# Weight loads moved to ScalarE's queue and gated-head stores to GpSimd's queue in a differential-attention layer

## The chip, the cores and the metric

The kernel runs on one core of one Trainium2 chip. The core has five engines that each run their own list of instructions in order: TensorE (PE in the profile), VectorE (DVE), ScalarE (ACT), GpSimd (POOL) and SyncE (SP). A transfer between HBM and on-chip memory is started by an instruction in one of these lists, and is then carried out by 16 DMA engines. An instruction that waits for a semaphore holds everything behind it in the same list. The metric is the device time of one execution in microseconds (us); lower is better.

## What is computed

One layer of gated differential attention, for 1024 tokens, width 1024, 16 heads of 128 columns each (two maps of 64), in float32:

```python
h = rms_norm(x, norm_g)
q, k, v, z = jnp.split(h @ w_in, 4, axis=-1)
q = rms_norm(q.reshape(b, s, DA_HEADS, 2, DA_HEAD), q_norm_g) * (DA_HEAD ** -0.5)
k = rms_norm(k.reshape(b, s, DA_HEADS, 2, DA_HEAD), k_norm_g)
...
    probs = jax.nn.softmax(scores + bias[None, :, None], axis=-1)
    weights = probs[:, :, 0] - lam * probs[:, :, 1]
    outs.append(jnp.einsum('bhqk,bkhe->bqhe', weights.astype(v.dtype), vb))
...
o = rms_norm(o, head_norm_g) * (1.0 - lam_0)
o = o.reshape(b, s, BRANCH) * jax.nn.silu(z)
return x + o @ w_out
```

`scores` is causal with a linear bias by distance.

## The kernel before

Float32 products are made from float16 pairs: each operand is split into a high and a low part, and three matmuls (high x high, high x low, low x high) stand for one.

The kernel works head by head, in the order of `heads`: the eight odd heads, then the eight even ones. For each head, `project` makes queries, keys and values (`gemm_piece`, L365 to L367: eight pieces of 128 tokens, each in one of three PSUM banks of the pool `ps_g`) and the gate (`gate`, L442 to L452, two halves `c` of 512 tokens; z is stored in a buffer `sz`, of which there are three). Heads 10, 12 and 14 (`LATE`) get their gates in `late_gates` at the end. At the same time, `attend` does the attention of the head before: eight steps of `scores`, each for 128 queries and 128 to 1024 keys (matmuls L564; VectorE takes the scores from PSUM with a running minimum, L553; ScalarE takes the exponential, L570; VectorE combines the two maps, L573 to L576; ScalarE and VectorE split the result, L66 and L580; a transposing transfer L582 on SyncE's queue turns it for `values`). `merge` interleaves the two lists by estimated TensorE time.

The weights of a head come from `w_in` in `load_raw`: eight transfers (`L135`), one for each 128 rows, into the buffer `raww`, of which there is one. A transfer is 256 KB for four blocks (q, k, v, z) and 192 KB for three. `split_w` then takes each block's largest square on ScalarE (L159), finds a scale, and splits: ScalarE writes the high part (L197); VectorE the low part of q and k (L203); GpSimd that of v and z (L200 scales in place, L201 subtracts). So the load for the next head can only start when the last L201 has read `raww`.

A finished half of a head (`finalize`) is gated on GpSimd (`L532`), or on VectorE for the late heads, and is stored to `g_dram` (`L533`, 256 KB). That store frees the `sz` buffer, for which a later `L447` waits. At the end the heads are read back and multiplied by `w_out` (L493 to L499).

A scheduler orders each engine's list when the program is built, by a simulated timeline; instructions that `pin` or `keep_in_program_order` marks keep their place. So moving a transfer to another queue also changes the order around it.

Of the kernel before, what the change touches and what calls it, by code (L numbers as in the profile page):

```python
# [39 lines left out]
def diff_attention_kernel(  # L40
# [18 lines left out]
    V, A, G, T, Q = nc.vector, nc.scalar, nc.gpsimd, nc.tensor, nc.sync  # L59
# [22 lines left out]
    g_dram = [dram.tile([4, P, NH, P], F32, name=f"g_dram{c}") for c in range(2)]  # L82
# [22 lines left out]
    heads = [h for h in range(NH) if h % 2 == 1] + [h for h in range(NH) if h % 2 == 0]  # L105
    place = {h: i for i, h in enumerate(heads)}

    with ExitStack() as main:
# [16 lines left out]
        def load_raw(hd, raw=None, blocks=None):  # L125


            if blocks is None:
                blocks = range(3 if isinstance(hd, slice) or hd in LATE else 4)
            if raw is None:  # L130
                raw = wr.tile([P, KT, 4, P], F32, name="raww", tag="raww")
            for k in range(KT):
                rows = wq_view[k * P:(k + 1) * P]
                bs = slice(blocks[0], blocks[-1] + 1)
                ins = Q.dma_start(raw[:, k, bs], rows[:, 3, hd] if isinstance(hd, slice) else rows[:, bs, hd])  # L135
                if hd == heads[0]:
                    tc.keep_in_program_order(ins)
            return raw, blocks
# [75 lines left out]
        with ExitStack() as pro:  # L214
# [12 lines left out]
            load_x()  # L227
            A.dma_start(gb, bcast(norm_g))
            raw0 = load_raw(heads[0], None, range(3))[0]
            load_x()  # L230
            load_x()
# [35 lines left out]
            for t in range(NB):  # L267
                ht = hts[t]
                c, o = t // 4, (t % 4) * P
# [7 lines left out]
                if t == 0:  # L277
                    for _ in range(KT + 1):
                        next(w0)
                    hts.append(chain(1))  # L280
                    for _ in w0:
                        pass
                    load_raw(heads[0], raw0, range(3, 4))
# [65 lines left out]
        def project(hd, wt, st):  # L349
# [46 lines left out]
            if nx is not None:  # L396
                st["wt"] = {}
                prep.append(split_w(*load_raw(nx), st["wt"], nx))
# [106 lines left out]
        def late_gates(sts, wt):  # L505
            for c in range(2):
                wo = wo_half(0, wr, "rawo", 2) if c else None
                if c:
                    g01 = qkp.tile([P, 2, 2, 4, P], F32R, name="gt01", tag="qk")
                    for q in range(2):  # L510
                        raw = tmp.tile([P, 4, 2, P], F32, name="rawg", tag="rw", bufs=2)
                        first.update(split_g(g01[:, q], raw.rearrange("p a b e -> p (a b) e"), 0, q))
                for n, (hd, st) in enumerate(sts):
                    for k in gate(st, wt, n, c):
                        if c == 1 and k % 3 == 0:
                            next(wo, None)
                        yield 0.64
                    if n < len(sts) - 1:
                        finalize(hd, c, st["t"][c], st["z"][c])
            yield from part_block(tmp.tile([P, 1024], F32, name="xr0", tag="sqk", bufs=2)[:, :512], 0, 0, first)  # L520
# [3 lines left out]
        def finalize(hd, c, t1, z):  # L524
            if hd == heads[-1]:
                V.tensor_tensor(t1, t1, z, ALU.mult)
                gs = glast[c]
                V.tensor_scalar(gs[0], t1, 1.0, None, ALU.mult)
                V.tensor_tensor(gs[1], t1, gs[0].bitcast(F32), ALU.subtract)
                return  # L530
            e = V if hd in LATE else G
            e.tensor_tensor(z, t1, z, ALU.mult)  # L532
            Q.dma_start(g_dram[c][:, :, place[hd], :].rearrange("t p e -> p t e"), z.rearrange("p (t e) -> p t e", t=4))  # L533

        def attend(hd, st):

# [73 lines left out]
            def head_norm(c):  # L610
                os, sq, sqh, sql = pos["n"]
                pm_ = ps_o.tile([P, 512], F32, name="pmn", tag="po")
                T.matmul(pm_, ones, sqh, start=True, stop=False)
                T.matmul(pm_, ones, sql, start=False, stop=True)
                yield 0.43
                A.activation(sq, pm_, AF.Ln, bias=eps_t)
                A.activation(sq, sq, AF.Exp, scale=-0.5)
                if hd in LATE[:-1]:
                    nm = ("whz", "wlz")[c]
                    t1 = wzp.tile([P, 512], F32, name="t1", tag=nm)  # L620
                    st["t"].append(t1)
                    V.scalar_tensor_tensor(out=t1, in0=os, scalar=gh, in1=sq, op0=ALU.mult, op1=ALU.mult)
                else:
                    V.scalar_tensor_tensor(out=sq, in0=os, scalar=gh, in1=sq, op0=ALU.mult, op1=ALU.mult)  # L624
                    finalize(hd, c, sq, st["z"][c])
# [36 lines left out]
        for i in range(NH + 1):  # L662
            att = None
            if i > 0:
                hd, stp = prev
# [81 lines left out]
```

## Time and profile before

| | us |
|---|---|
| median of three runs (1170.47 to 1178.97) | 1173.36 |
| the profiled execution's own time | 1169.15 |
| its span in the trace | 1167.4 |
| TensorE busy (95% of the span) | 1109.9 |
| VectorE busy (78%) | 906.5 |
| ScalarE busy (64%) | 751.7 |
| GpSimd busy (23%) | 269.7 |

Busy time does not count instructions that start transfers or wait. In a row of the timeline the first number is the start in us from the span's start, the second the time in us; "[1.02 <-DVE v_k L95]" is the idle time of that engine just before the row, and what ended it. SPq and ACTq are the lists of SyncE and ScalarE where they start transfers. The middle of the trace, from about 170 to 870 us, repeats with each head, about 58 us for one.

### The profile page before, as it was taken

To read this page: it belongs to the slowest core of one execution; us is meant where nothing else is said; L and a number is where in the kernel's file an instruction comes from. 1 tells how busy PE (TensorE), PEld (TensorE's weight loads), DVE (VectorE), ACT (ScalarE), POOL (GpSimd) and SP (SyncE) were. 2 spreads that over 40 slices of the span, in tenths; PEclk is the share of its full clock that TensorE was granted. 3 is DMA by queue.
4 is the path that set the end of the run, shared out by engine and by line. 5 is a ranking of instruction groups with operands and counts; after the bars stand their busy time and mean duration, and the time that the engine had idled before them with its cause. 6 is when DMAs were issued, how large, how long until landed. Compare 5 with 4: busy or idle time off the path is not lost.

```text
span 1167.4 us, 18462 instructions
## 1 busy us (share of the span) xinstructions
PE 1109.9 (95%) x6154; PEld 670.2 (57%) x6154; DVE 906.5 (78%) x2336; ACT 751.7 (64%) x1585; POOL 269.7 (23%) x208
## 2 busy tenths in 40 slices
PE   4999999999899999999999999999999988999998
PEld 3655554555455555554545555555555535788887
DVE  6868968898879898989888989797898898554121
ACT  4757678686868686868686868686768766230000
POOL 2221313131413131314131313212120402022000
PEclk7999999999999999999999999999999988999999
DMA  6352636354636364635473635353664456766341
GB/s 222 109 118 57 147 82 143 81 125 96 142 84 141 86 144 83 150 77 145 82 150 77 147 80 136 79 142 70 138 136 91 116 112 160 193 235 227 113 131 70
DMA packets 327887, 143.50 MB, mean 123 GB/s; under 512 B 225136, under 2 KB 307312, under 8 KB 327792
## 3 DMA queue, kind: packets, MB, share of 16 engines
q1 hardware_dynamic: 323040, 133.93, 47.8%
q10 hardware_dynamic: 4752, 8.39, 2.6%
q8 instruction: 48, 0.79, 0.3%
q14 instruction: 47, 0.39, 0.1%
HBM read 63.11 MB, written 16.25 MB: 68 GB/s over the span
## 4 chain that ended last, share of the span: by engine, by line
PE 53%; DVE 15%; ACT 11%; DMA 7%; issue 6%; POOL 4%; SPq 4%; ACTq 0%; DVEq 0%; POOLq 0%
PE pg L365 8%; PE pg L366 8%; PE pg L367 8%; PE pf L493 5%; PE pf L494 5%; PE pf L495 5%; DMA raww<-in_l_w_in_dram 4%; DVE p L553 4%; SPq L135 3%; PE pss L564 3%; ACT wsp L197 3%; ACT wsp L159 3%; POOL wsp L201 2%; ACT p L570 2%; DVE p L576 2%
## 5 line engine op out<-in xcount | busy, mean ns | idle before, releaser
L365 PE MATMUL pg<-wsp,h 128*128 128x384 f16 x1024 | 336.1, 328 | 12.8 <-DVE sz L452 7.7
L366 PE MATMUL pg<-wsp,h 128*128 128x384 f16 x1024 | 336.1, 328 | 1.2 <-POOL wsp L201 1.2
L367 PE MATMUL pg<-wsp,h 128*128 128x384 f16 x1024 | 336.0, 328 | 0.9 <-DVE h L276 0.9
L570 ACT ACTIVATE p<-p,mn 128x128 f32<-128x128 f32 (+7 forms) x256 | 196.6, 769 | 36.1 <-DVE mn L553 36.0
L564 PE MATMUL pss<-qk 128*128 128x512 f16 (+3 forms) x768 | 165.9, 327 | 18.5 <-DVE mn L553 18.5
L553 DVE CUSTOM_DVE_ANT_0 p<-pss,toep,nsl 128x512 f32<-128x512 f32 (+3 forms) x256 | 161.3, 643 | 17.7 <-DMA wt<-p 8.2
L66 ACT ACTIVATE p<-p,rc 128x128 f16<-128x128 f32 (+7 forms) x128 | 98.8, 773 | 77.6 <-DVE p L576 71.7
L366 PEld LDWEIGHTS <-h 128*128 128x128 f16 x1024 | 100.8, 98 | 77.3 <-issue 17.2
L367 PEld LDWEIGHTS <-h 128*128 128x128 f16 x1024 | 100.8, 98 | 68.7 <-issue 4.0
L365 PEld LDWEIGHTS <-h 128*128 128x128 f16 x1024 | 100.7, 98 | 65.9 <-issue 3.7
L580 DVE SCALAR_TENSOR_TENSOR p<-p,rc,p 128x128 f16<-128x128 f32 (+7 forms) x128 | 109.1, 853 | 10.2 <-ACT p L66 9.4
L564 PEld LDWEIGHTS <-qk 128*128 128x128 f16 x768 | 70.8, 98 | 78.6 <-issue 26.6
L576 DVE SCALAR_TENSOR_TENSOR p<-p,rc,p 128x128 f32<-128x128 f32 (+7 forms) x128 | 108.7, 854 | 0.0
L607 POOL TENSOR_TENSOR sql<-sqo,sqh 128x512 fp32r<-128x512 f32 x30 | 41.0, 1366 | 263.2 <-ACT sqh L605 263.2
L442 PE MATMUL pz<-h,wsp 128*128 128x512 f16 x256 | 98.1, 383 | 1.8 <-DVE sz L452 1.8
L444 PE MATMUL pz<-h,wsp 128*128 128x512 f16 x256 | 98.1, 383 | 0.0
L443 PE MATMUL pz<-h,wsp 128*128 128x512 f16 x256 | 98.1, 383 | 0.0
L200 POOL TENSOR_SCALAR raww<-raww,scw 128x1024 f32<-128x1024 f32 (+1 forms) x31 | 43.5, 1410 | 178.4 <-ACT wsp L197 137.2
L532 POOL TENSOR_TENSOR sz<-sqo,sz 128x512 f32<-128x512 f32 x26 | 33.7, 1295 | 184.9 <-DVE sqo L624 165.4
L159 ACT ACTIVATE wsp<-raww 128x1024 f16<-128x1024 f32 x61 | 63.7, 1045 | 19.3 <-DMA raww<-in_l_w_in_dram 14.9
L553 DVE CUSTOM_DVE_ANT_0 p<-pss,toep,mn 128x128 f32<-128x128 f32 (+3 forms) x128 | 75.4, 603 | 0.3 <-PE pss L564 0.3
L201 POOL TENSOR_TENSOR wsp<-raww,wsp 128x1024 f16<-128x1024 f32 (+1 forms) x31 | 71.7, 2327 | 0.5
(159 smaller groups left out, 2048.7 us busy)
## 6 DMA issues: line engine op xcount, KB each, us to landing
raww<-in_l_w_in_dram SPq DMA_DIRECT2D x96, 256.0 KB, 4.3
rawo<-in_l_w_out_dram SPq DMA_DIRECT2D x32, 256.0 KB, 4.7
qk<-qk SPq DMA_DIRECT2D x64, 128.0 KB, 2.3
raww<-in_l_w_in_dram SPq DMA_DIRECT2D x40, 192.0 KB, 3.6
g_dram<-sz SPq DMA_DIRECT2D x30, 256.0 KB, 2.2
rawg<-g_dram ACTq DMA_DIRECT2D x24, 256.0 KB, 4.0
xt<-in_x_dram SPq DMA_DIRECT2D x8, 512.0 KB, 5.2
xr<-in_x_dram SPq DMA_DIRECT2D x16, 256.0 KB, 3.5
```

The source lines that it names most:

```text
L66: A.activation(out, in_, AF.Copy, scale=scale)
L159: A.activation(hi[:, :, s_], raw[:, :, s_], AF.Square, accum_out=bd[:, j:j + 1])
L365: T.matmul(pg, a_h, w_h, start=k == 0, stop=False)
L366: T.matmul(pg, a_h, w_l, start=False, stop=False)
L367: T.matmul(pg, a_l, w_h, start=False, stop=k == KT - 1)
L442: T.matmul(pz, wt["hi"][:, k, n], hh[c][:, k], start=k == 0, stop=False)
L443: T.matmul(pz, wt["hi"][:, k, n], hl[c][:, k], start=False, stop=False)
L553: V.tensor_tensor_reduce(out=pm[m][:, o:o + w], in0=pss[:, :w], in1=toep[:, u:u + w], scale=nslope, scalar=3e38 if prev[m] is None else pr ...
L564: T.matmul(pss[m][:, :w].rearrange("p (t q) -> p t q", q=P), qk[:, c, 0, i % 4, m], qk[:, b, v, :w // P, m], start=v == 1, stop=v == 2)
L570: A.activation(pm[m][:, :n], pm[m][:, :n], AF.Exp, scale=-1.0, bias=prev[m], accum_out=sx[:, m:m + 1])
L576: V.scalar_tensor_tensor(out=p0, in0=p1, scalar=rc[:, 1:2], in1=p0, op0=ALU.mult, op1=ALU.add)
L580: V.scalar_tensor_tensor(out=pl[:, n:], in0=p0, scalar=rc[:, 0:1], in1=pl[:, :n], op0=ALU.mult, op1=ALU.subtract)
```

## The change

Loads of `w_in` for all heads but the first are started by ScalarE (`A`) in place of SyncE (`Q`): 16 groups of eight transfers, 128 in all (96 of 256 KB, 32 of 192 KB; the last group holds the gate weights of the three late heads). The 30 stores of gated heads are started by GpSimd (`G`).

```diff
-                ins = Q.dma_start(raw[:, k, bs], rows[:, 3, hd] if isinstance(hd, slice) else rows[:, bs, hd])
+                ins = (Q if hd == heads[0] else A).dma_start(raw[:, k, bs], rows[:, 3, hd] if isinstance(hd, slice) else rows[:, bs, hd])
...
-            Q.dma_start(g_dram[c][:, :, place[hd], :].rearrange("t p e -> p t e"), z.rearrange("p (t e) -> p t e", t=4))
+            G.dma_start(g_dram[c][:, :, place[hd], :].rearrange("t p e -> p t e"), z.rearrange("p (t e) -> p t e", t=4))
```

ScalarE's list in the middle of the program, where the fifth attended head is at its seventh step (896 keys; `p_4107` and `p_4108` are the two maps' scores). Before:

```order
L570 ACTIVATE p_4107,sx<-p_4107,mn 128x896
L570 ACTIVATE p_4108,sx<-p_4108,mn 128x896
L97 ACTIVATE y_k<-v_k 128x16
L98 ACTIVATE y_k<-y_k 128x16
L447 ACTIVATE sz<-pz,inv 128x512
L66 ACTIVATE p_4108<-p_4107,rc 128x896
L449 ACTIVATE sz<-sz 128x512
```

The same place in ScalarE's list after the change:

```order
L570 ACTIVATE p_4107,sx<-p_4107,mn 128x896
L135 DMA raww<-in_l_w_in_dram 128x4x128 x2
L570 ACTIVATE p_4108,sx<-p_4108,mn 128x896
L135 DMA raww<-in_l_w_in_dram 128x4x128 x2
L97 ACTIVATE y_k<-v_k 128x16
L447 ACTIVATE sz<-pz,inv 128x512
L135 DMA raww<-in_l_w_in_dram 128x4x128
L98 ACTIVATE y_k<-y_k 128x16
L135 DMA raww<-in_l_w_in_dram 128x4x128 x2
L66 ACTIVATE p_4108<-p_4107,rc 128x896
L449 ACTIVATE sz<-sz 128x512
L135 DMA raww<-in_l_w_in_dram 128x4x128
```

Two of the eight loads now stand between the two exponentials of the step, and six more among the short operations behind them.

A little further in ScalarE's list (the gate's last exponential L451, the squares L159 of the weights just loaded, and L386, a part of the key's and query's split). Before:

```order
L386 ACTIVATE sqk<-rw 128x16x64
L617 ACTIVATE sqo<-sqo 128x512
L159 ACTIVATE wsp,bd<-raww 128x8x128 x3
L451 ACTIVATE sz<-sz 128x512
L159 ACTIVATE wsp,bd<-raww 128x8x128
L570 ACTIVATE p_4273,sx<-p_4273,mn 128x128
```

After:

```order
L617 ACTIVATE sqo<-sqo 128x512
L451 ACTIVATE sz<-sz 128x512
L159 ACTIVATE wsp,bd<-raww 128x8x128 x4
L386 ACTIVATE sqk<-rw 128x16x64
L570 ACTIVATE p_4273,sx<-p_4273,mn 128x128
```

L451 now comes ahead of all four squares, and L386 behind them.

VectorE's list at the first of these places (`rc` comes from the sums `sx` of the two exponentials; `p_4195` is the next step). Before:

```order
L553 ISA p_4108,mn<-pss,toep,mn,nsl 128x384
L553 ISA mn 128x1
L95 TENSOR_SCALAR v_k<-ssk,ep 128x8 x2
L573 RECIPROCAL rc<-sx 128x2
L553 ISA p_4195,mn<-pss,toep,nsl 128x512
L553 ISA mn 128x1
```

After:

```order
L553 ISA p_4108,mn<-pss,toep,mn,nsl 128x384
L553 ISA mn 128x1
L580 SCALAR_TENSOR_TENSOR p_3996<-p_3995,rc,p_3996 128x768
L95 TENSOR_SCALAR v_k<-ssk,ep 128x8 x2
L553 ISA p_4195,mn<-pss,toep,nsl 128x512
L553 ISA mn 128x1
L573 RECIPROCAL rc<-sx 128x2
```

L573, which needs both exponentials, now stands behind the next step's first L553.

In SyncE's list only the transposing transfers L582 and L388 and the copies L391 are left in the middle of the program. On GpSimd each L533 stands right behind its L532.

## Rows read from the trace of the kernel before

**Rows 1.** The page, busy us of each engine, share, instructions.

```profile
PE 1109.9 (95%) x6154; PEld 670.2 (57%) x6154; DVE 906.5 (78%) x2336; ACT 751.7 (64%) x1585; POOL 269.7 (23%) x208
```

**Rows 2.** Windows: stretch, length, busy PE, PEld, DVE, ACT, POOL, then clock, DMA.

```profile
0.00:100.00 100.00, 77.65 (x440) 48.83 (x441) 71.12 (x214) 60.66 (x141) 22.33 (x25) 0.88 0.49 136
...
170.00:870.00 700.00, 679.49 (x3966) 380.95 (x3965) 604.68 (x1606) 534.64 (x1130) 181.40 (x122) 1.00 0.51 114
870.00:1167.00 297.00, 282.81 (x1338) 200.37 (x1336) 172.27 (x372) 107.34 (x210) 47.78 (x50) 0.97 0.52 146
```

**Rows 3.** Waits of PE, 170 to 870 us: total us, times, longest.

```profile
PE pss L564 <- DVE mn L553: 9.8, 10, 1.6
PE pg L365 <- DVE sz L452: 7.3, 8, 1.9
```

**Rows 4.** Waits of DVE and of ACT for transfers, 170 to 870 us.

```profile
DVE p L553 <- DMA wt<-p: 5.0, 5, 2.2
...
ACT sz L447 <- DMA g_dram<-sz: 2.8, 4, 1.4
```

**Rows 5.** Waits of SyncE's queue, whole span: total us, times, longest.

```profile
SPq L533 <- POOL sz L532: 109.0, 17, 10.2
...
SPq L135 <- POOL wsp L201: 61.7, 16, 7.4
```

**Rows 6.** Lines L135, L533, L479: time to issue, ns min/median/max, first and last.

```profile
L135 SPq DMA_DIRECT2D raww<-in_l_w_in_dram x144: 328/622/2157, 1.2 to 871.4; - x144
...
L533 SPq DMA_DIRECT2D g_dram<-sz x30: 364/382/993, 124.8 to 992.0; - x30
...
L479 ACTq DMA_DIRECT2D rawg<-g_dram x32: 326/326/1071, 902.2 to 1138.9; - x32
```

**Rows 7.** Landing of the stores L533, us from issue, min/median/max.

```profile
DMA to landing us min/median/max: 2.2/2.2/3.5
```

**Rows 8.** Timeline of SyncE's queue, one head in the middle.

```profile
363.63 5.46 SPq L135 DMA_DIRECT2D raww<-in_l_w_in_dram  x8
...
379.64 0.54 SPq L533 DMA_DIRECT2D g_dram<-sz  x1
```

**Rows 9.** Timeline of POOL, the same head.

```profile
358.66 4.94 POOL L201 TENSOR_TENSOR wsp<-raww,wsp 128x1024 f16<-128x1024 f32 x2
...
376.64 1.27 POOL L532 TENSOR_TENSOR sz<-sqo,sz 128x512 f32<-128x512 f32 x1 [10.57 <-DVE sqo L624]
```

**Rows 10.** Timeline of ACT, the same head.

```profile
361.00 1.04 ACT L570 ACTIVATE p<-p,mn 128x896 f32<-128x896 f32 x1
...
362.73 1.04 ACT L570 ACTIVATE p<-p,mn 128x896 f32<-128x896 f32 x1 [0.59 <-DVE mn L553]
...
373.77 1.06 ACT L159 ACTIVATE wsp<-raww 128x1024 f16<-128x1024 f32 x1
...
376.91 0.61 ACT L451 ACTIVATE sz<-sz 128x512 f32<-128x512 f32 x1
...
382.21 0.69 ACT L447 ACTIVATE sz<-pz,inv 128x512 f32<-128x512 f32 x1
```

**Rows 11.** Timeline of DVE, the same head, behind the two exponentials.

```profile
364.77 0.15 DVE L573 RECIPROCAL rc<-sx 128x2 f32<-128x2 f32 x1
364.84 0.73 DVE L553 CUSTOM_DVE_ANT_0 p<-pss,toep,nsl 128x512 f32<-128x512 f32 x1
```

**Rows 12.** Timeline of PE, the same head, its only waits.

```profile
377.01 1.02 PE L564 MATMUL pss<-qk 128*128 128x512 f16 x4 [0.78 <-DVE mn L553]
378.36 0.32 PE L365 MATMUL pg<-wsp,h 128*128 128x384 f16 x1 [0.32 <-DVE sz L452]
```

**Rows 13.** Timeline of ACT and then PE, first head.

```profile
51.36 1.06 ACT L159 ACTIVATE wsp<-raww 128x1024 f16<-128x1024 f32 x1 [1.64 <-DMA raww<-in_l_w_in_dram]
...
56.06 0.19 ACT L97 ACTIVATE y_x<-v_x 128x1 f32<-128x1 f32 x1
...
59.66 0.66 PE L273 MATMUL tp<-ident,htok 128*128 128x128 f32 x2 [2.13 <-DVE htok L257]
```

## The prediction, made before the changed kernel was run

> **What bounds the kernel now.** I read the page's busy times first. TensorE works 1109.9 of 1167.4 us [rows 1], so a change of loads and stores can win only what TensorE stands still. The windows say where that is [rows 2]: in the middle, 170 to 870 us, TensorE works 679.49 of 700 us, so 20.5 us of idle time in all lie there; in the first 100 us it is idle for 22.35, in the last 297 for 14.2. The column for VectorE shows the second limit: 604.68 of 700 us in the middle (86%), ScalarE 534.64 (76%), GpSimd only 181.40 (26%). An engine that gets later by a microsecond is therefore not at once on the path, but VectorE has little room.
>
> Then the waits, for what the moved transfers hold up. TensorE in the middle waits 9.8 us for VectorE's running minimum L553 (`mn`) and 7.3 us for VectorE's L452, which frees a bank of the gate [rows 3]; the rest up to 20.5 is short pieces. None of the two is a wait for a transfer. VectorE waits 5.0 us for transposed weights and ScalarE 2.8 us for a store of a gated head, both in the middle [rows 4]. SyncE's own queue does wait much: 109.0 us in 17 waits at the stores L533, for GpSimd's L532, and 61.7 us in 16 waits at the loads L135, for GpSimd's last L201 [rows 5]. These are the waits that the change removes from SyncE. But behind them only [rows 4] shows anyone late, 5.0 + 2.8 us, and those two are not the bound.
>
> **The loads, on ScalarE.** 128 loads move in 16 groups of eight. On SyncE eight of four blocks took 5.46 us to issue [rows 8], 0.68 us each. With 192 KB in place of 256 I take 0.51 by the ratio. The total is 96 x 0.68 + 32 x 0.51 = 82 us of a second queue's time, 5.1 us a group. ScalarE, 76% busy in the middle, has 165 us left there, so the sum fits; the question is where in its list it lies.
>
> Take the head at 361 us. GpSimd's two L201 run from 358.66 for 4.94 us and so end at 363.60 [rows 9]. ScalarE ran the first 896-key exponential from 361.00 to 362.04, waited 0.59 us for VectorE and ran the second from 362.73 to 363.77 [rows 10]. In the new list two loads stand between them (the first order rows in the section on the change). They wait for L201, till 363.60, then take 2 x 0.68 = 1.37 us; the second exponential runs from 364.97 to 366.01, 2.2 us later. Queued behind the wait are this exponential, then the key norm's L97, L447, L66 and L449; of these the exponential is wanted first. VectorE's L573 needs both exponentials' sums. Before, it ran at 364.77, ahead of the 512-key L553, which ended at 364.84 + 0.73 = 365.57 [rows 11]. In the new list L573 stands behind that L553, so it would be ready for L573 at 365.5 and gets it at 366.0: VectorE is late by 0.5 us a group. The other six loads go among short operations, 4.1 us in which ScalarE issues; L66 and the transposed weights that follow from it are needed some steps later by `values`, so I put nothing on the path for them.
>
> The bounds: the fastest plain load on ScalarE's own list, L479, took 326 ns to issue [rows 6]. With 0.33 in place of 0.68 the second exponential ends at 363.60 + 0.66 + 1.04 = 365.3, ahead of L573, and the cost is 0. If on the other side all 2.2 us reach TensorE, it is 16 x 2.2 = 35. I take VectorE's lateness in full, 16 x 0.5 = +8, since VectorE, at 86%, has little slack to give it back, and the shapes in question (four blocks by 128 columns in 128 rows) are those of L135's row, not L479's.
>
> **What the loads free on SyncE.** Transposes and copies no longer stand behind the wait for L201. The most that this can win is VectorE's wait for transposed weights and ScalarE's for the store [rows 4], 5.0 + 2.8, so 0 to −8. TensorE names neither, and what it names is VectorE, which gets its weights earlier only where [rows 4] shows it late. I take 0.
>
> **The order.** The build moves two things. L451, the gate's last exponential, stood behind three squares L159 and now stands ahead of all. Before, the squares began at 373.77 and L451 ran at 376.91 [rows 10]; TensorE then waited 0.32 us at 378.36 for L452, which follows L451 [rows 12]. With L451 about three squares (3.2 us) earlier, that wait goes. Of the 7.3 us of its kind [rows 3] I take most, −5, with 0 (the gates meet another full bank) and −7.3 as bounds. The other short wait of that place, 0.78 us for `mn` at 377.01 [rows 12], is VectorE's, and the term above has it. I don't credit a shorter wait for `mn`: nothing in the change takes work off VectorE.
>
> **The stores, on GpSimd.** 30 stores move. At this head GpSimd's L532 ran from 376.64 to 377.91 [rows 9], but SyncE issued L533 only at 379.64 [rows 8], 1.73 late. SyncE's issue takes 0.38 and the store lands 2.2 us after its issue, at most 3.5 [rows 6, 7]; here that is about 382. The next L447, which rewrites the buffer, began at 382.21 [rows 10]: it was just in time. After, the store can be issued at 377.91. No row shows a transfer that GpSimd starts. From below, SyncE's price: landing at 377.91 + 0.38 + 2.2 = 380.5, and even the 2.8 us of [rows 4] go, but as TensorE doesn't wait for them that is 0. From above, its issue costs as much as a whole L532, 1.27, and the landing is the slowest, 3.5: 377.91 + 1.27 + 3.5 = 382.7, 0.5 late. Sixteen heads less the three late ones make 13 whose gate can meet such a store, so 13 x 0.5 = +7. I take 0, since the 1.73 us that SyncE was late pays for any price up to that. The issue itself lies in GpSimd's gaps (10.57 us ahead of that L532).
>
> The Trainium skill speaks for a price near the lower end: "DMA: Bandwidth & Descriptors", section "Anatomy of one DMA — SWDGE (gpsimd) path", fits about 2.0 us and the bytes at 436 GB/s for such a transfer. By it 256 KB would take some 2.6 us, an estimate, and the store would land at 380.5; the sum would be the same.
>
> **The first head.** The first group's loads now stand in ScalarE's list among the setup. L159 at 51.36 already waited 1.64 us for its load, the norm's L97 ran at 56.06, and TensorE waited 2.13 us for `htok` at 59.66, at the end of that chain [rows 13]. A load that stands ahead of this chain, with up to three issues of 0.68, makes it later by 0 to 2; a second group soon after may hold the first attention steps up by as much again, 0 to 3. I take +2 of 0 to +5. At the end, where the heads are read back, I take 0: the late heads' stores come long before they are read.
>
> **The sum.** 8 (loads on ScalarE) + 0 (SyncE) − 5 (order) + 0 (stores) + 2 (first head) = +5 us. Against its own profiled execution, 1169.15 us (span 1167.4 and 1.8 around it), that is 1174. That execution lies 4.2 below the median of the runs shown, 1173.36, against which I forecast 1178.
>
> **The rivals.** All times are on the median; 1% of it is 11.7 us, about what a measurement of this kernel can tell from no change.
>
> A, ScalarE held. The wait for GpSimd and the issues reach TensorE beyond VectorE's 0.5. Half of the 35 us gives 1173 + 18 = 1191, all of it 1208. It decides from about 1 us a group carried, 16 us. For it: the load can't be issued before L201 ends, and ScalarE's list is in order. Against: ScalarE is idle a quarter of the middle.
>
> B, slower by the stores. If GpSimd's stores land later than 382.21, L447 waits at the head of ScalarE's list, and the exponentials behind it with it. From the bound above, 382.7, each further microsecond is 13 us: 1 us late gives 1186, 2 us 1199. For it: at this head the landing was just in time. Against: 1.73 us of earlier issue. A rule of the Trainium skill would do this: "DMA: Bandwidth & Descriptors", section "SWDGE vs HWDGE vs iDMA", says that GpSimd writes the descriptors of its transfers into state that VectorE can lock it out of, while transfers started by SyncE or ScalarE are immune; no row of before shows such a wait.
>
> C, faster. The new order and the free SyncE take away TensorE's idle time in the middle: half of 20.5 gives 1163, all of it 1153. It decides the other way from 57% of it (11.7 of 20.5). For it: all of the waits at L135 and L533 [rows 5] leave the list of the transposes. Against: the two waits that make up most of the 20.5 are for VectorE, which gets no less work.
>
> That the change does nothing, as no one waits for SyncE, gives 1173 and lies inside the forecast.
>
> **How the numbers follow.** Forecast, within 1%: 0.55. A 0.17, nearly all over 1%. B 0.13, all but a fraction over 1%. C 0.15, of which about half is over 1%. So faster 0.08, slower 0.32 (0.17 + 0.13, and 0.02 for the forecast's own upper edge, which touches the 1%), same 0.60, the rest. The likeliest one's own range is 1168 to 1185. The range for 8 in 10 ends below at 1163, C with half of the idle time won, and above at 1192, just past A with half of its price and B with 1.5 us late; what lies outside is about half of A, of B and of C, some 0.2.
>
> **What would show it.** L135's issue time in ScalarE's list (0.33 or 0.68), and two loads between the two 896-key exponentials, the second starting about 4.0 us after the first (364.97 against 361.00). TensorE's wait for `mn` up from 9.8, its wait for L452 down from 7.3; their sum against the 20.5 us of idle time in the middle. SyncE's waits at L135 and L533 gone. The issue and landing of GpSimd's L533, and ScalarE's wait for the store against 2.8: above some 10 us B holds. In the first head, TensorE's wait at 59.66. I am wrong if ScalarE waits at the loads for much longer than in this head's 1.6 us (363.60 less 362.04), because the build put them earlier, or if TensorE's idle time in the middle falls below 12 us.

## The result, and the profile after

The changed kernel takes 1215.97 us (median of six runs, 1213.06 to 1222.32) against 1171.92 for the kernel before (six runs): a ratio of 1.0372, with a 95% interval of 1.0335 to 1.0409. The forecast of 1178 and its range up to 1192 were wrong: the change costs 44 us.

The page's busy times of the changed kernel, to be read beside [rows 1]:

```profile
PE 1125.9 (93%) x6154; PEld 675.7 (56%) x6154; DVE 906.6 (75%) x2336; ACT 757.7 (63%) x1585; POOL 297.7 (25%) x238
```

The span is 1212.0 us in place of 1167.4. TensorE has the same 6154 matmuls, yet is busy 16.0 us longer; the other 28.6 us of the 44.6 are more idle time (1212.0 − 1125.9 = 86.1, before 57.5). The windows of the same stretches as in [rows 2] (length, busy PE, PEld, DVE, ACT, POOL, clock, DMA):

```profile
0.00:100.00 100.00, 77.76 (x442) 49.22 (x443) 70.15 (x203) 58.58 (x134) 23.38 (x25) 0.88 0.49 134
170.00:870.00 700.00, 661.48 (x3779) 368.03 (x3777) 571.81 (x1521) 513.72 (x1072) 195.61 (x141) 0.98 0.52 108
870.00:1212.00 342.00, 319.57 (x1545) 220.77 (x1542) 205.74 (x465) 135.40 (x275) 59.78 (x61) 0.97 0.54 140
```

In the middle TensorE is idle 38.5 us where it was 20.5, and its granted clock is 0.98 where it was 1.00. Waits of TensorE over the whole span, then two of VectorE's (total us, times, longest):

```profile
PE pg L365 <- DVE vl L419: 30.9, 11, 4.9
PE pss L564 <- DVE mn L553: 16.0, 12, 4.2
...
PE pg L365 <- DVE sz L452: 5.6, 6, 1.3
```

```profile
DVE br L164 <- ACT wsp L159: 33.6, 13, 5.2
DVE p L553 <- DMA wt<-p: 16.3, 10, 5.2
```

The wait for L553 is no longer than before (18.5 us over the span), and that for L452 is shorter (7.7), the way that was forecast. New is the first row (1.6 us in two waits before): about once a head, TensorE finds no free bank of `ps_g`, because VectorE's L419 has not taken the last part of a piece out of it. And VectorE waits long at L164 (18.8 us before), for the squares L159 that read the loaded weights.

**One head in the changed kernel.** It is the same head as in [rows 8 to 12]; its L201 ends at 372.8. VectorE's timeline, with rows left out:

```profile
388.19 0.47 DVE L553 CUSTOM_DVE_ANT_0 p<-pss,toep,nsl 128x256 f32<-128x256 f32 x1
...
390.87 0.17 DVE L164 TENSOR_SCALAR br<-bd 128x4 fp32r<-128x4 f32 x1 [2.20 <-ACT wsp L159]
391.82 1.23 DVE L387 TENSOR_TENSOR sqk<-rw,sqk 128x1024 f16<-128x1024 f32 x1 [0.78 <-ACT sqk L386]
...
394.93 0.28 DVE L419 SCALAR_TENSOR_TENSOR vl<-pg,vh 128x128 f16<-128x128 f32 x1
```

VectorE stands still for 2.20 us at L164, then 0.78 for L386, then does 1.23 us of L387 ahead of what TensorE wants. TensorE's timeline there, and the windows over its idle time and behind it:

```profile
395.27 0.48 PE L365 MATMUL pg<-wsp,h 128*128 128x384 f16 x1 [3.86 <-DVE vl L419]
395.54 0.53 PE L366 MATMUL pg<-wsp,h 128*128 128x384 f16 x1
```

```profile
391.40:395.30 3.90, 0.04 (x2) 0.03 (x1) 3.44 (x9) 3.90 (x13) 0.00 (x0) 0.89 0.32 74
395.30:397.30 2.00, 2.00 (x7) 0.98 (x7) 2.00 (x9) 2.00 (x7) 0.00 (x0) 0.50 1.15 253
397.30:400.00 2.70, 2.70 (x10) 1.22 (x8) 2.64 (x8) 1.86 (x5) 0.00 (x0) 0.50 0.96 216
```

After 3.86 us without work the granted clock is 0.50, the lower of its two levels (1.2 GHz), and a matmul of this shape takes 0.53 us; the mean of the 1024 of L365 over the program is 0.334. Such a wait is thus mostly paid for twice, though not each time: of the eight waits for L419 of over 2 us from 273 to 705 us, seven are followed by matmuls at 0.50, and after the one of 3.33 us at 273 the clock stays at 1.00. All in all the mean granted clock is 0.966 in place of 0.982, and 16.0 us more of busy time stand beside 28.6 of idle time.

**Why the squares are late.** L135 in that group, first of before (363 us), then of the changed kernel (372 us): the issue in ns (min/median/max), and the time from issue to landing in us.

```profile
L135 SPq DMA_DIRECT2D raww<-in_l_w_in_dram x8: 609/628/769, 363.6 to 368.5; - x8
...
DMA to landing us min/median/max: 3.1/4.7/5.2
```

```profile
L135 ACTq DMA_DIRECT2D raww<-in_l_w_in_dram x8: 547/650/1886, 372.8 to 378.8; - x8
...
DMA to landing us min/median/max: 3.1/7.1/7.7
```

The median issue is hardly dearer (650 ns against 628, with one of the eight at 1886), but the loads land later. At 374.89, amid them, SyncE starts the transposing transfer of the 768-key step:

```profile
L582 SPq DMA_TRANSPOSE wt<-p x1: 2168/2168/2168, 374.9 to 374.9; - x1
...
DMA to landing us min/median/max: 8.6/8.6/8.6
```

It takes 8.6 us to land; the median of all 128 is 3.1. Before, that transfer had been issued at 359.53, ahead of the loads, and landed in 3.2. The last of the eight loads lands 13.4 us after L201's end in the six middle heads from 372 us on (10.2 before).

### The profile page after: what moved, and what is told of

Same layout as the page of the kernel before. It is cut to its first block, busy times and chain, and to the rows that moved or that the text cites. A ratio compares the mean times of both kernels' runs of the same rounds, so it can differ in the third digit from the quotient of the medians.

```text
span 1212.0 us, 18424 instructions
## 1 busy us (share of the span) xinstructions
PE 1125.9 (93%) x6154; PEld 675.7 (56%) x6154; DVE 906.6 (75%) x2336; ACT 757.7 (63%) x1585; POOL 297.7 (25%) x238
## 4 chain that ended last, share of the span: by engine, by line
PE 40%; DVE 23%; ACT 14%; DMA 11%; issue 9%; ACTq 1%; POOL 1%; SPq 0%; DVEq 0%; POOLq 0%
DMA raww<-in_l_w_in_dram 8%; PE pg L365 6%; PE pg L366 6%; PE pg L367 6%; DVE p L553 5%; PE pf L493 5%; PE pf L494 5%; PE pf L495 5%; ACT wsp L197 4%; ACT p L570 3%; ACT wsp L159 3%; DVE p L576 3%; DVE p L580 3%; DVE sqk L387 2%; PE pss L564 2%
## 5 line engine op out<-in xcount | busy, mean ns | idle before, releaser
L365 PE MATMUL pg<-wsp,h 128*128 128x384 f16 x1024 | 342.2, 334 | 43.0 <-DVE vl L419 30.9
L366 PE MATMUL pg<-wsp,h 128*128 128x384 f16 x1024 | 342.1, 334 | 1.2 <-POOL wsp L201 1.2
L367 PE MATMUL pg<-wsp,h 128*128 128x384 f16 x1024 | 341.9, 334 | 0.0
L564 PE MATMUL pss<-qk 128*128 128x512 f16 (+3 forms) x768 | 168.5, 329 | 17.4 <-DVE mn L553 16.0
L553 DVE CUSTOM_DVE_ANT_0 p<-pss,toep,nsl 128x512 f32<-128x512 f32 (+3 forms) x256 | 161.4, 643 | 31.0 <-DMA wt<-p 16.3
L366 PEld LDWEIGHTS <-h 128*128 128x128 f16 x1024 | 102.2, 100 | 109.1 <-issue 50.7
L365 PEld LDWEIGHTS <-h 128*128 128x128 f16 x1024 | 102.3, 100 | 72.9 <-issue 8.6
L367 PEld LDWEIGHTS <-h 128*128 128x128 f16 x1024 | 102.5, 100 | 70.9 <-issue 9.1
L576 DVE SCALAR_TENSOR_TENSOR p<-p,rc,p 128x128 f32<-128x128 f32 (+7 forms) x128 | 116.1, 907 | 0.0
L580 DVE SCALAR_TENSOR_TENSOR p<-p,rc,p 128x128 f16<-128x128 f32 (+7 forms) x128 | 108.5, 850 | 7.8 <-ACT p L66 7.6
L607 POOL TENSOR_TENSOR sql<-sqo,sqh 128x512 fp32r<-128x512 f32 x30 | 46.6, 1552 | 255.0 <-ACT sqh L605 255.0
L159 ACT ACTIVATE wsp<-raww 128x1024 f16<-128x1024 f32 x61 | 63.7, 1047 | 36.1 <-DMA raww<-in_l_w_in_dram 27.0
L532 POOL TENSOR_TENSOR sz<-sqo,sz 128x512 f32<-128x512 f32 x26 | 35.5, 1365 | 179.6 <-DVE sqo L624 174.2
L553 DVE CUSTOM_DVE_ANT_0 p<-pss,toep,mn 128x128 f32<-128x128 f32 (+3 forms) x128 | 76.4, 604 | 0.0
L201 POOL TENSOR_TENSOR wsp<-raww,wsp 128x1024 f16<-128x1024 f32 (+1 forms) x31 | 73.4, 2382 | 0.5
```

The costliest lines, as they stand in the source:

```text
L159: A.activation(hi[:, :, s_], raw[:, :, s_], AF.Square, accum_out=bd[:, j:j + 1])
L365: T.matmul(pg, a_h, w_h, start=k == 0, stop=False)
L366: T.matmul(pg, a_h, w_l, start=False, stop=False)
L367: T.matmul(pg, a_l, w_h, start=False, stop=k == KT - 1)
L553: V.tensor_tensor_reduce(out=pm[m][:, o:o + w], in0=pss[:, :w], in1=toep[:, u:u + w], scale=nslope, scalar=3e38 if prev[m] is None else pr ...
L564: T.matmul(pss[m][:, :w].rearrange("p (t q) -> p t q", q=P), qk[:, c, 0, i % 4, m], qk[:, b, v, :w // P, m], start=v == 1, stop=v == 2)
```

## The experiments

Most kernels here separate the two things that the edit does: it moves transfers to other queues, and it lets the build order all five lists anew. For that the program is built twice. From a first build, with other queues, the order of each engine's list is read off; in the second, each instruction is chained behind its predecessor of that order, with no wait of its own:

```diff
+        for engine in ('PE', 'DVE', 'Activation', 'Pool', 'SP') if order else ():
+            last = None
+            for i in (traced[j] for j in order[engine]):
+                if str(i.engine).endswith("." + engine):
+                    if last is not None:
+                        tc.add_manual_dep(i, last.name, mybir.DependencyInfo(
+                            mybir.DependencyClass.NoSync, mybir.DependencyReason.DATA), reason="order")
+                    last = i
```

A transfer that is on another queue in the first build is not chained; the scheduler places it. `LOADS` and `STORES` name the queues; the second line of a pair is that of the build whose order is taken. In these kernels lines stand a few numbers lower in the file (L553 is L555, L558, L561 or L565); the tiles' names tell them. A ratio is to the kernel before on the same chip, with its 95% interval.

### Queue or order

**queues_alone**: order of before, queues of the changed kernel.

```diff
+LOADS, STORES = "scalar", "gpsimd"
...
+    (LOADS, STORES), kept = ("sync", "sync"), (LOADS, STORES)
```

> Loads on ScalarE's list and stores on GpSimd's as in the changed kernel, but every other instruction of all five engines stands in the order of the kernel before (forced when the program is built). Theory 1, the queues: the time comes from the loads landing later after GpSimd's last L201 (about 13 us in the changed kernel, 10 before) and from the squares L159 that wait for them; then this is as slow as the changed kernel, +35 to +50 us on before, with the same landing. Theory 2, the order: the new lists of VectorE, ScalarE and TensorE cost the time and the queues nothing; then this is within 6 us of before.

**order_alone**: the reverse.

```diff
+LOADS, STORES = "sync", "sync"
...
+    (LOADS, STORES), kept = ("scalar", "gpsimd"), (LOADS, STORES)
```

> All loads and stores on SyncE's queue as before, but every other instruction of all five engines stands in the order of the changed kernel (forced when the program is built). Theory 1, the queues: within 6 us of before, loads landing about 10 us after L201. Theory 2, the order: +35 to +50 us, with TensorE's wait for L419 once a head as in the changed kernel (30.9 us in all).

queues_alone measured 1.0211 (1.0176 to 1.0245), order_alone 1.0152 (1.0115 to 1.0190). Neither theory is right alone: 2.1% + 1.5% = 3.6%, and the change measured 3.7%. Both have their clock part, busy times of queues_alone and of order_alone:

```profile
PE 1121.7 (94%) x6154; PEld 674.2 (57%) x6154; DVE 909.0 (76%) x2336; ACT 752.2 (63%) x1585; POOL 293.6 (25%) x238
```

```profile
PE 1118.8 (94%) x6154; PEld 674.4 (57%) x6154; DVE 909.5 (77%) x2336; ACT 756.2 (64%) x1585; POOL 273.7 (23%) x208
```

Of their 23.6 and 18.6 us of longer span, 11.8 and 8.9 are busy time. Where it goes shows in the stretches between the ends of the last L201 before the third, sixth, twelfth and sixteenth moved group of loads, us against before:

| stretch | before | changed | queues_alone | order_alone |
|---|---|---|---|---|
| to the third group | 136.2 | +2.8 | +2.2 | +3.6 |
| to the sixth | 166.3 | +5.4 | +5.8 | +2.2 |
| to the twelfth | 351.8 | +20.5 | +10.8 | +6.5 |
| to the sixteenth | 210.1 | +8.2 | +3.3 | 0.0 |
| to the end | 302.9 | +7.8 | +1.6 | +6.3 |

The two add up as a total, and not stretch by stretch: 5.8 against 2.8 in the first, 3.3 against 8.2 in the fourth. So the sum doesn't show that the changed kernel pays the same two costs; where they differ comes below. TensorE's waits for L419, L553 and L452 in order_alone, over the whole span:

```profile
PE pg L367 <- DVE vl L421: 24.6, 11, 4.0
PE pss L566 <- DVE mn L555: 8.2, 9, 2.2
...
PE pg L367 <- DVE sz L454: 1.7, 3, 0.8
```

### Loads or stores

**loads_only** and **stores_only** each make one line of the change, with the order that the build gives; **loads_queue** and **stores_queue** make the same with the order of before.

```diff
-                ins = Q.dma_start(raw[:, k, bs], rows[:, 3, hd] if isinstance(hd, slice) else rows[:, bs, hd])
+                ins = (Q if hd == heads[0] else A).dma_start(raw[:, k, bs], rows[:, 3, hd] if isinstance(hd, slice) else rows[:, bs, hd])
```

> Only the loads are moved to ScalarE; stores stay on SyncE. The lists differ little from the changed kernel's. Both theories: if the loads carry the change, +35 to +50 us. If the stores carry it (GpSimd's transfers slow down the loads, or L447 waits for them), within 6 us of before.

> Order of before, loads on ScalarE, stores on SyncE as before. If the loads carry all of the cost of the queues: +20 to +25 us, like queues_alone. If half of it is the stores on GpSimd: +10 to +14 us.

```diff
-            Q.dma_start(g_dram[c][:, :, place[hd], :].rearrange("t p e -> p t e"), z.rearrange("p (t e) -> p t e", t=4))
+            G.dma_start(g_dram[c][:, :, place[hd], :].rearrange("t p e -> p t e"), z.rearrange("p (t e) -> p t e", t=4))
```

> Only the stores are moved to GpSimd; loads stay on SyncE. If the loads carry the change, within 6 us of before; the store is issued within 1 us of its L532 and lands about 2.9 us after that. If the stores carry it, +35 us or more.

> Order of before, stores on GpSimd, loads on SyncE as before. If the loads carry all of the cost of the queues: within 4 us of before. If half of it is the stores: +10 to +14 us. With the stores' natural order (stores_only) it was 1.1% slower, with TensorE's waits of 4.0 and 4.2 us at 953 and 958 us; if those are of the order, they are gone here.

The loads carry it: 1.0346 (1.0320 to 1.0373) with their order, 1.0183 (1.0146 to 1.0220) without. The stores cost nothing by themselves, 0.9988 (0.9967 to 1.0009). stores_only's 1.0107 (1.0078 to 1.0136) is then the order: its last stretch, with the late heads' gates, is 14.7 us longer, while that of stores_queue is 1.5 shorter.

### The exponential behind the load

**loads_behind**: as queues_alone, with one more chain (`SECOND[hd, 6]` is the second exponential of the 896-key step, `LOADED` the eight loads of a head).

```diff
+        for n in range(5, 13) if order else ():
+            for load in LOADED[heads[n + 1]]:
+                tc.add_manual_dep(load, SECOND[heads[n - 2], 6].ins.name, mybir.DependencyInfo(
+                    mybir.DependencyClass.NoSync, mybir.DependencyReason.DATA), reason="order")
```

> As queues_alone (order of before, loads on ScalarE, stores on GpSimd), but in the eight heads where a load stood between the two 896-key exponentials all eight loads stand behind the second one. Theory a: it is the wait for L201 ahead of the second exponential that costs; then TensorE's wait for L553 falls from 29.4 to about 19 us, and the time from +24 to +5 to +12 us. Theory b: it is the landing, or the issue among the later operations; the loads start 1 to 2 us later, so it stays at +20 us or gets slower.

It measured 1.0108 (1.0066 to 1.0150), +13 us in place of +24. In queues_alone, ScalarE, VectorE and TensorE at the head of [rows 9 to 12] show the wait that the prediction had spoken of:

```profile
372.92 1.04 ACT L572 ACTIVATE p<-p,mn 128x896 f32<-128x896 f32 x1
375.54 0.55 ACTq L137 DMA_DIRECT2D raww<-in_l_w_in_dram  x1
376.19 1.04 ACT L572 ACTIVATE p<-p,mn 128x896 f32<-128x896 f32 x1 [2.14 <-POOL wsp L203]
```

```profile
377.36 0.17 DVE L575 RECIPROCAL rc<-sx 128x2 f32<-128x2 f32 x1 [0.60 <-ACT p L572]
```

```profile
390.03 1.02 PE L566 MATMUL pss<-qk 128*128 128x512 f16 x4 [1.86 <-DVE mn L555]
```

L201 ends at 375.50, so some 1.5 of the 2.14 us are the wait for it and the rest is the issue of one load. VectorE is late by 0.60 us, and TensorE then waits 1.86 where it waited 0.78. ScalarE waits so at seven of the 16 groups, the seventh to the thirteenth (1.98 to 2.14 us). In loads_behind the same three places:

```profile
374.46 1.04 ACT L575 ACTIVATE p<-p,mn 128x896 f32<-128x896 f32 x1 [0.59 <-DVE mn L558]
375.36 0.55 ACTq L138 DMA_DIRECT2D raww<-in_l_w_in_dram  x1
```

```profile
376.50 0.15 DVE L578 RECIPROCAL rc<-sx 128x2 f32<-128x2 f32 x1
```

```profile
388.86 1.02 PE L569 MATMUL pss<-qk 128*128 128x512 f16 x4 [0.88 <-DVE mn L558]
```

The exponential is on time and the wait is back to 0.88. From the end of L201 at 375.3 to that at 666.6 us, five heads, it takes 291.2 us, as before (290.8); queues_alone takes 297.7. So eight issues on ScalarE among its short operations cost nothing there; the wait ahead of an exponential, with one issue behind it, does. My number for TensorE's whole wait was wrong, though: it fell only from 30.7 to 27.8 us. The profiled span is still 15.3 us longer than before. Of these 8.6 lie ahead of the sixth group, in heads whose loads I didn't move: the stretch from the third group to the sixth is 6.9 us longer, and there transposing transfers fall among the loads, which land 14.4 us after L201 (mean of the fourth to the sixth group) in place of 11.8. Another 3.2 lie between the sixth group and the seventh, and 3.1 behind the twelfth.

### L387 behind the wait for the squares

**split_back**: order_alone, with L386 put back ahead of the squares that stand right before it, and L387 ahead of L164 (`br`).

```diff
+    for engine, key in (("Activation", "squares"), ("DVE", "br")):
+        line = order[engine]
+        for j in [j for j in line if j in at["split"]]:
+            k, first = line.index(j), None
+            while line[k - 1] in at[key]:
+                k, first = k - 1, line[k - 1]
+            if first is not None:
+                line.remove(j)
+                line.insert(line.index(first), j)
```

> The order of the changed kernel with all transfers on SyncE (as in order_alone), but ScalarE's L386 is put back ahead of the four squares L159 and VectorE's L387 back ahead of L164. Theory a: the order costs because L387 (1.22 us) stands behind L164, which waits for the load, and holds up L419, which empties a bank for TensorE; then TensorE's wait for L419 (21.8 us in order_alone) falls below 5 us and the time is no more than before, and perhaps 5 to 10 us less, as L451 is still ahead of the squares. Theory b: other moves of the order cost; then it stays at +12 to +20 us.

**split_back_moved**: the same edit on the changed kernel.

> The changed kernel with its own queues; only ScalarE's L386 is put back ahead of the squares L159 and VectorE's L387 ahead of L164. On SyncE's queue the same edit took 9 of 15 parts in a thousand away. Theory a: the costs of order and queue add; then this is 25 to 35 us slower than before in place of 44. Theory b: with the loads as late as they are here, L164 alone holds VectorE up and L387 costs nothing; then it stays at +40 us or more.

split_back measured 1.0061 (1.0040 to 1.0082) against 1.0152 for order_alone. VectorE in order_alone (first two rows) and in split_back:

```profile
383.88 0.17 DVE L166 TENSOR_SCALAR br<-bd 128x4 fp32r<-128x4 f32 x1 [0.52 <-ACT wsp L161]
384.82 1.22 DVE L389 TENSOR_TENSOR sqk<-rw,sqk 128x1024 f16<-128x1024 f32 x1 [0.78 <-ACT sqk L388]
```

```profile
380.58 1.22 DVE L395 TENSOR_TENSOR sqk<-rw,sqk 128x1024 f16<-128x1024 f32 x1
381.71 0.16 DVE L172 TENSOR_SCALAR br<-bd 128x4 fp32r<-128x4 f32 x1
```

The 1.22 us lie in time that VectorE would have waited. TensorE's wait for L419 at this place falls from 2.16 to 1.36 us, and the six heads to the twelfth group take 349.2 us, 2.6 less than before. But I had expected this wait to vanish and the whole to be no slower; 20.9 of 24.6 us of it stay over the span. Most of what came back is the clock: between the two profiled spans, 1186.0 and 1171.1 us, lie 9.3 us of TensorE's busy time and 5.6 of idle time, and the mean granted clock is 0.974 and 0.981. The loads still land 12.0 us after L201 in the six middle heads (12.1 in order_alone, 10.2 before), as a transposing transfer stands between loads four and five; whether the wait that is left comes from that was not tested. What is left of the time, +0.6% by the ratio, lies in the first two stretches and the last (+2.9, +1.3 and +2.2 us in the profiled run), which I didn't take apart. split_back_moved is 1.0269 (1.0228 to 1.0309), 10 in a thousand under the changed kernel, as theory a had it: the cost is there with the late loads too.

### The transpose among the loads

**transposes_wait**: the changed kernel, order and queues, with one true wait more (`TURNED[hd, 5]` is the transposing transfer of the 768-key step).

```diff
+        for n in range(5, 13) if order else ():
+            for load in LOADED[heads[n + 1]]:
+                tc.add_manual_dep(TURNED[heads[n - 2], 5].ins, load.name, mybir.DependencyInfo(
+                    mybir.DependencyClass.Sync, mybir.DependencyReason.DATA), reason="order")
```

> The changed kernel in its own order and with its own queues; in eight heads the transposing transfer of the 768-key step, which SyncE now starts in the middle of the eight loads, waits until all of them have landed. Theory a: transposes in flight slow the loads down; then the eight loads land about 10 to 11 us after L201 in these heads in place of 12.7 to 14.5, TensorE's wait for L419 falls from 30.9 to below 20 us, and the time by 8 to 20 us, less what the late transposes cost VectorE. Theory b: loads that ScalarE starts are slow by themselves; then they land as late as in the changed kernel and the time is the same or longer.

It measured 1.0237 (1.0201 to 1.0272), some 16 us less than the changed kernel, though it adds waits. One group of loads in it:

```profile
L138 ACTq DMA_DIRECT2D raww<-in_l_w_in_dram x8: 547/580/652, 374.9 to 380.8; - x8
...
DMA to landing us min/median/max: 3.1/3.7/4.8
```

3.7 us in place of 7.1: loads that ScalarE starts are as fast as SyncE's, when no transpose is in flight beside them. The last one lands 10.0 us after L201 (13.4), and TensorE's wait for L419 falls from 30.9 to 11.0 us:

```profile
PE pg L370 <- DVE vl L424: 11.0, 8, 3.7
```

The stretch to the twelfth group is 5.6 us longer than before in place of 20.5.

**three_undone**: split_back_moved, transposes_wait and loads_behind together, on the changed kernel.

> The changed kernel with its own queues, and three edits together: L386 and L387 back ahead of the squares and of L164 (split_back_moved, alone 1.0269), the 768-key transpose held until the loads have landed in eight heads (transposes_wait, alone 1.0237), and the loads that stood between two exponentials put behind the second one. Theory a: these three are what the change costs in the middle of the program; then TensorE's waits there fall to before's and what is left, some 8 to 16 us, lies in the first and the last heads, which the edits do not touch. Theory b: ScalarE's issue itself, or its queue, costs as well; then it stays above +20 us, with waits once a head in the middle.

It is slow: 1.0343 (1.0303 to 1.0384). That is above the +20 us of theory b, but the run doesn't show theory b's reason. The loads land 11.0 us after L201 (10.0 in transposes_wait): they start behind the exponential, 1.04 us after L201 in place of 0.03. So the held transposes land later still, and VectorE waits longer for the buffers that they read (of `p` there are three for each map). Its waits, and one of them:

```profile
DVE p L565 <- DMA wt<-p: 34.7, 16, 5.1
```

```profile
448.70 0.35 DVE L565 CUSTOM_DVE_ANT_0 p<-pss,toep,nsl 128x128 f32<-128x128 f32 x1 [2.67 <-DMA wt<-p]
```

Over the span this wait was 8.2 us before (5.0 in the middle, [rows 4]), 16.3 in the changed kernel and 26.2 in transposes_wait. The span of three_undone is 8.7 us longer than that of transposes_wait, 6.0 of it busy time of TensorE; that VectorE's longer wait is the cause of this is likely and not shown. So the run says nothing on what ScalarE's issue costs; holding the transposes is a probe, not a remedy. A fourth `p` buffer was not tried.

No version here beats the kernel before. stores_queue equals it.

## Why the prediction was wrong

**The order** (−5 forecast, bounds 0 to −7.3) is the step that failed most: by itself it costs 18 us (1.0152), 23 more than the step says, where the whole forecast of +5 was 39 short of the 44. Its gain came: in order_alone TensorE's wait for L452 fell to 1.7 us over the span (7.7 before), and that for L553, for which I had credited nothing, to 8.2 (18.5 before). The step says that the build moves two things and works out one. What I left out stood in the order rows: L386 behind the four squares on ScalarE, so VectorE's L387 behind L164. I read what had moved ahead, and not what had moved behind an instruction that waits for a load. order_alone's wait for L419 is 24.6 us; split_back took nine of the fifteen parts in a thousand back; what the other six are is open.

**What the loads free on SyncE** (0, bounds 0 to −8) had the wrong sign in the changed kernel. In the six middle heads it takes both halves of the change. With the order of before (queues_alone) the transposing transfer of the 768-key step is still issued ahead of the loads, and the last load lands 10.4 us after L201. With the new order on one queue (order_alone) it stands between loads four and five, and the last lands at 12.1. With both, as VectorE's L580 of that step is later (second order rows for VectorE), it starts amid the loads of another queue, and the last lands at 13.4 (10.2 before). Taking it away gave 16 us back (transposes_wait). These 16 us overlap the 18 of the order and the 21 of the loads below; the three don't add. I had counted who waits for SyncE's list, and not what its order had kept apart. The Trainium skill says in "Trainium Kernel Development and Optimization", section "Key Constraints", that transfers of SyncE, ScalarE and GpSimd run on the same 16 DMA engines and interleave, so that several issuing engines save issue time alone. The landing of 7.1 us against 3.7 agrees with the interleaving.

**The loads on ScalarE** (+8, bounds 0 to 35): the mechanism is there with the order of before, and not in the changed kernel. With the order of before the loads cost about 21 us (loads_queue). At the head that I worked out, VectorE's lateness of 0.5 us was measured as 0.60, but TensorE's wait grew by 1.08 and not by 0.5, and the clock adds to it. ScalarE waits so at seven groups, where I counted 16. In the changed kernel ScalarE reaches the exponentials later, with L201 over by then, and the loads issue while they run (the median of 128 is 0.548 us). Between the two exponentials it waits 0.91 to 1.46 us in the fifth to the thirteenth group, each time for VectorE's L553 and never for L201; at the head of [rows 8 to 12] the second starts 2.06 us after the first, and not 4.0. So the term's mechanism plays no part there: the transposes and L387 are what the runs show to cost time.

**The clock** was no term at all. [rows 2] showed 1.00 in the middle, and I priced waits at their length. 16.0 of the 44.6 us are more busy time for the same matmuls, with a mean granted clock of 0.966 in place of 0.982.

**The stores** (0): right, as the step had it. GpSimd's L533 over the program:

```profile
L533 POOL DMA_DIRECT2D g_dram<-sz x30: 757/806/957, 125.0 to 1029.7; - x30
...
DMA to landing us min/median/max: 2.5/2.9/4.7
```

An issue of 0.81 us and a landing of 2.9 lie inside the two bounds (1.27 and 3.5), and ScalarE's wait for the store, 2.8 us in [rows 4], is gone. Rival B did not happen, and with no issue above 0.96 us no row shows the lock-out that the prediction cites. The Trainium skill's fit in "DMA: Bandwidth & Descriptors", section "Anatomy of one DMA — SWDGE (gpsimd) path", gave an estimate of 2.6 us; the median landing is 0.3 longer.

**The first head** (+2) measured +2.8 to the third group, within its bounds; with the order alone it is +3.6, so that it fits may be luck. **The end** (0) measured +7.8; with the order alone it is +6.3, so it is mostly the late heads' new order. Why it costs I did not test.

**The rivals.** A's 18 us for half of its price is near the 21 us of the loads with the order of before. In the changed kernel ScalarE is not held by L201, so A did not happen there, and the order, which I had put on the other side of the sum and into rival C, costs about as much. Alone, queues_alone and order_alone would have come out near 1198 and 1191 on the median of 1173.36, on either side of the range's upper end. Neither of my two signs of being wrong came: ScalarE did not wait longer at the loads, and TensorE's idle time in the middle rose to 38.5 us, where I had looked for a fall below 12.

What stays open: what keeps 20.9 us of the wait for L419 in split_back, and how the 24 parts in a thousand that transposes_wait leaves divide between L387, the first heads and the late heads. The edits overlap (each makes the squares' lateness matter less), and three_undone, which should have told, brought a wait of its own.

## What to carry to other kernels

Where a scheduler orders the lists, the order is half of an edit: read in the new lists what now stands behind an instruction that waits for a transfer, on every engine, and not only what came ahead. A load that has to wait for its buffer belongs behind the operations that others want at that time, if it is issued by a busy engine: in queues_alone the wait ahead of an exponential was the cost, and issues among short operations were free. And before a queue is relieved, look at what its order kept apart: here a transpose and a stream of loads on two queues slowed each other down. Two halves of a change that add up as totals need not be what the whole pays for.

## What the runs showed of the hardware

- A transposing transfer started beside eight 256 KB loads of another queue took 8.6 us to land (3.2 before, ahead of the loads), and the loads 7.1 (3.7 without it). On one queue, with the transpose between loads four and five (order_alone), the median load landed in 3.6 to 4.4 us in the six middle heads; there the eight issues were spread over 6.8 to 8.6 us, from the first start to the last, in place of 4.6 to 5.0.
- After 3.86 us without a matmul TensorE's granted clock was 0.50 for the next microseconds (0.53 us a matmul in place of 0.33); after 0.78 to 1.86 us, in the rows above, matmuls kept their length. The length of a wait alone doesn't tell: in the changed kernel the clock stayed at 1.00 after one of 3.33 us (at 273 us), and in queues_alone it was 0.50 from 509.1 to 512 us, behind two waits of 1.56 and 0.72 us.
- GpSimd starts a 256 KB store in 0.81 us, 0.40 us after the operation that it waits for, and it lands 2.9 us after its issue; SyncE's landed in 2.2 [rows 7].
